# RWKV-7's chunked recurrence in 64x64 tiles of the array, both heads of a pair at once

## The chip, the cores and the metric

One core of one Trainium2 chip runs one launch of one decoder layer (batch 1, 1024 tokens, model width 1024, float32 in and out). The metric is the device time of the launch in microseconds (us).

## The reference

```python
for l in range(DEPTH):
    h = rms_norm(x, norm_mix_pre[l])
    proj = h @ w_in[l]                      # r,k,v and low ranks | S5 input | two gates
    o_rwkv = rwkv7_branch(...) @ w_branch_rwkv[l]
    o_s5 = s5_branch(...) @ w_branch_s5[l]
    mixed = (g_rwkv * o_rwkv + g_s5 * o_s5) @ w_out[l]
    x = x + rms_norm(mixed, norm_mix_post[l])
    f = conv_ffn(rms_norm(x, norm_ffn_pre[l]), ...)
    x = x + rms_norm(f, norm_ffn_post[l])
```

The part that matters is the recurrence inside rwkv7_branch, for 8 heads of width 64 (state S of 64x64 a head):

```python
def step(S, inp):
    r_t, w_t, k_t, v_t, a_t, b_t = inp
    sa = einsum('bhij,bhj->bhi', S, a_t)
    S = S * w_t[:, :, None, :] + sa[..., None] * b_t[:, :, None, :] + v_t[..., None] * k_t[:, :, None, :]
    return S, einsum('bhij,bhj->bhi', S, r_t)
```

## The kernel before

The layer runs in stages: input projection and the S5 scan, then the RWKV recurrence, then the merge, the output projection, the feed-forward part. Large products are split into three (high and low halves of both operands, lines 171 to 173, tile gm in the recurrence's stage).

**The recurrence.** The 1024 tokens go in two halves of 512 (th) and the 8 heads in four pairs of 128 channels; a unit d takes two pairs (u = 0, 1), so four heads, of one half. There are four units. A half has eight chunks (c) of 64 tokens. For each chunk the delta rule becomes products of 64x64 matrices: rwkv_front builds decayed rows ar (a part in columns 0 to 63, r part in 64 to 127) and bk (b part, k part), and the masked Gram matrices gr of bk with ar; the b-a block of gr has to be inverted (unit lower triangular). The inverse goes in blocks of 32: rwkv_inv takes the 32x32 diagonal blocks through DRAM (md, xd) and solves them in 62 VectorE steps; rwkv_level joins two blocks by two small products (lines 783, 786). rwkv_nat turns bk and v into token-major layout (lines 731, 738, 740). rwkv_chain then walks the eight chunks: state products (814), products with v (816), the solve (824), the outputs (828) and the new state (832, 835). rwkv_out is the layer norm and the gate.

In the kernel before, U (the solved rows, partitions 0 to 63) and v (partitions 64 to 127) share the tile UV, so one product over 128 rows takes both; gr has the b part on partitions 0 to 63 and the k part on 64 to 127, for both heads of a pair alike. Products are written to chk (two banks of PSUM) and chb.

**What sets the order.** TensorE's order is the order of emission. A planner (`drive`) walks lanes, which are generators: one chain lane (rwkv_nat, rwkv_level, rwkv_chain, rwkv_out of unit after unit) and two preparing lanes (rwkv_front of u = 0 and 1, then rwkv_inv). A lane yields (its cost in us, the wait until it may go on, a factor). Between a lane's steps the planner issues background steps of 0.68 us, three products each (gates, then merge and output projection): as many as the wait asks for, and as the lane's cost times 0.8 asks for. The other engines' queues are ordered by the framework by priority, and each runs in order.

```python
T_KN, T_BK, T_GR, T_INV, T_LV, T_CH, T_LN = 5.0, 9.0, 2.5, 36.0, 1.0, 0.8, 11.0
```

Of the kernel before, what the change touches and what calls it, by code (L numbers as in the profile page):

```python
# [9 lines left out]
F32 = mybir.dt.float32  # L10
# [3 lines left out]
ALU = mybir.AluOpType  # L14
# [10 lines left out]
CDEC = math.exp(-0.5)  # L25
MAGIC = 1.5 * 2.0 ** 23
# [44 lines left out]
class Kern:  # L71
# [569 lines left out]
    def rwkv_front(self, d, u):  # L641

        nc, V, G, A = self.nc, self.nc.vector, self.nc.gpsimd, self.nc.scalar
        mm = nc.tensor.matmul
# [51 lines left out]
        for q in range(2):  # L696
            ps = [self.rp((128, 4, 128)) for h in range(2)]
            for c in range(4 * q, 4 * q + 4):
                for h, sl in ((0, slice(0, 64)), (1, slice(64, 128))):
                    mm(ps[h][:, c % 4], bk[sl, c], ar[sl, c], start=c % 4 == 0, stop=True, skip_group_check=True)  # L700
            for h in range(2):
                V.tensor_tensor(d["gr"][:, u, 4 * q:4 * q + 4, h], ps[h], gm, ALU.mult)
            yield 1.8, T_GR
        g16 = d["gr"][:, u].rearrange("p c h t -> p (c h) t")
        for blk in range(2):
            sl = slice(32 * blk, 32 * blk + 32)
            nc.gpsimd.dma_start(d["md"][u, blk].rearrange("c q t -> q c t"), g16[sl, :, sl])
# [9 lines left out]
    def rwkv_nat(self, d):  # L717

        nc, A = self.nc, self.nc.scalar
        mm = nc.tensor.matmul  # L720
        ident = self.cst("ident")
        o = slice(d["th"] * 512, d["th"] * 512 + 512)
        d["bkn"] = self.tg("bkn", 1, (128, 2, 8, 128))
        d["UV"] = self.tg("UV", 1, (128, 8, 2, 2, 64))
        nc.gpsimd.memset(d["UV"][0:64], 0.0)
        for u in range(2):
            v = d["v"][u]
            for q in range(2):
                ps = self.rp((128, 4, 128))
                for c in range(4):  # L730
                    nc.tensor.transpose(ps[:, c], d["bk"][:, u, 4 * q + c], ident)
                A.copy(d["bkn"][:, u, 4 * q:4 * q + 4], ps)
                yield 0.5, 0
                ps = self.rp((128, 4, 128))
                for c in range(4):
                    b = 4 * q + c
                    if b == 0:
                        mm(ps[64:128, c], v[:, 0:64], ident, start=True, stop=True, skip_group_check=True)
                    else:
                        nc.tensor.transpose(ps[:, c], v[:, 64 * b - 64:64 * b + 64], ident)  # L740
                A.copy(d["UV"][64:128, 4 * q:4 * q + 4, :, u], ps[64:128].rearrange("p c (h i) -> p c h i", i=64))
                yield 0.5, 0.8

    def rwkv_inv(self, d):
# [19 lines left out]
        for u in range(2):  # L764
            xd = xds[:, u]

            g16 = d["gr"][:, u].rearrange("p c h t -> p (c h) t")
            for blk in range(2):
                sl = slice(32 * blk, 32 * blk + 32)
                nc.gpsimd.dma_start(g16[sl, :, sl], xd[16 * blk:16 * blk + 16].rearrange("c s r t -> (s r) c t"))  # L770

    def rwkv_level(self, d):
# [3 lines left out]
        g16 = [d["gr"][:, u].rearrange("p c h t -> p (c h) t") for u in range(2)]  # L776
        p0 = self.chk(1).rearrange("p (u c t) -> p u c t", u=2, t=32)
        p0, p1 = [p0[:, u] for u in range(2)], [self.chb().rearrange("p (c t) -> p c t", t=32) for u in range(2)]
        xz = [self.tg("ld", NLD)[0:64].rearrange("p (c t) -> p c t", t=32) for u in range(2)]
        for u in range(2):  # L780
            V.transpose(xz[u][0:32], g16[u][0:32, :, 0:32])
        yield 0, T_LT
        steps = ((lambda u, c: mm(p1[u][32:64, c], g16[u][0:32, c, 32:64], xz[u][0:32, c], start=c == 0, stop=True,
                                  skip_group_check=True),
                  lambda u: A.copy(xz[u][32:64], p1[u][32:64])),
                 (lambda u, c: mm(p0[u][0:32, c], xz[u][32:64, c], g16[u][32:64, c, 32:64], start=c == 0, stop=True,
                                  skip_group_check=True),
                  lambda u: A.copy(g16[u][0:32, :, 32:64], p0[u][0:32])))
        for step, evict in steps:
            for u in range(2):  # L790
                for c in range(16):
                    step(u, c)
                    if c % 8 == 7:
                        yield 0.4, 0.3, 4.5
                evict(u)
            yield 0, T_LV

    def rwkv_chain(self, d):
# [3 lines left out]
        S, pt, UV, gr, ar, bkn = self.S[d["g"]], d["pt"], d["UV"], d["gr"], d["ar"], d["bkn"]  # L802
        d["yn"] = self.tg("yn", 1, (128, 4, 2, 2, 64))
        kw = dict(stop=True, skip_group_check=True)
        uh = [(u, h) for h in range(2) for u in range(2)]
        for c in range(8):
            py = self.chk(1).rearrange("p (h n) -> p h n", h=2)[:, :, 0:128].rearrange("p h (u i) -> p h u i", i=64)
            cb = self.chb()
            pu = cb[0:64, 0:256].rearrange("p (h u i) -> p h u i", u=2, i=64)
            psn = cb[:, 256:384].rearrange("p (u i) -> p u i", i=64)  # L810
            for u in range(2):
                for h in (1, 0):
                    sl = slice(64 * h, 64 * h + 64)
                    mm(py[:, h, u], ar[sl, u, c], S[sl, u], start=u == 0, **kw)
            for u, h in uh:
                mm(py[0:64, h, u], gr[:, u, c, h, 0:64], UV[:, c, h, u], start=False, **kw)
            p1 = self.small.tile([64, 2, 2, 64], F32, tag="p1", name=self.nm("p1"), bufs=1)
            A.copy(p1, py[0:64])
# [3 lines left out]
            yield 1.25, T_CH  # L822
            for j, (u, h) in enumerate(uh):
                mm(pu[:, h, u], gr[0:64, u, c, h, 0:64], p1[:, h, u], start=j == 0, **kw)
            V.tensor_copy(UV[0:64, c], pu)
            yield 0.5, T_CH
            for u, h in uh:
                mm(py[64:128, h, u], gr[:, u, c, h, 64:128], UV[:, c, h, u], start=False, **kw)
            o = 64 * (c % 2)
            A.copy(d["yn"][o:o + 64, c // 2].rearrange("p u h i -> p h u i"), py[64:128])  # L830
            for u, h in uh:
                mm(psn[64 * h:64 * h + 64, u], bkn[:, u, c, 64 * h:64 * h + 64], UV[:, c, h, u],
                   start=u == 0 and h == 1, **kw)
            for u in range(2):
                V.scalar_tensor_tensor(S[:, u], psn[:, u], pt[:, c, u:u + 1], spt[:, u], ALU.mult, ALU.add)
            yield 0.9, T_CH
# [1008 lines left out]
```

## Time and profile before

| | |
|---|---|
| time, median of 3 runs | 1641.32 us |
| runs | 1638.31 to 1647.14 us |
| span of the profiled execution | 1644.6 us |
| instructions in it | 22694 |

The profiled execution is one more run of the same program; its own time is its span, 1644.6 us. Its page lists busy times of the engines: PE is the matrix engine, PEld its weight loads, DVE the vector engine, ACT the scalar engine, POOL GpSimd, SP the queue that issues most transfers. "L814" is line 814 of the kernel before. In the timeline a row has the start in us from the span's beginning, the duration in us, engine, line, operation, tiles (out<-in), then rows*columns of the array and the shape, and the number of instructions merged into the row. A row of groups has busy time and mean ns of one, then the engine's idle time before them and who ended it. A row of waits has who waited for whom, us in total, times, and the longest. A float32 matmul shows as two instructions, each with its own weight load.

### The profile page before, as it was taken

Reading aid. Unit: us, or ns where it says so; the run is one execution under the profiler, and the core shown is the slowest. Engines: PE = TensorE matmul, PEld = TensorE weight load, DVE = VectorE, ACT = ScalarE, POOL = GpSimd, SP = SyncE. Lnnn points to the kernel's source line nnn. Section 1 sums busy time; section 2 is a strip of 40 time slices with the busy share of each in tenths; the row PEclk is TensorE's granted clock in tenths of the full one; section 3 lists DMA queues with packets and bytes.
Section 4 is the critical chain, followed back from the end, with each engine's and each line's share of the span. In section 5 each row is a group of like instructions: output and inputs, shape, how many; then the busy total and the mean of one; then the engine's idle time right before and its main releaser. Section 6 shows DMA issues by size and latency. Waiting matters only on the chain. (4 is left out here: it accounts for less than half of the span.)

```text
span 1644.6 us, 22694 instructions
## 1 busy us (share of the span) xinstructions
PE 1542.0 (94%) x8372; PEld 1240.8 (75%) x8372; DVE 1132.4 (69%) x2035; ACT 699.6 (43%) x1069; POOL 134.6 (8%) x190
## 2 busy tenths in 40 slices
PE   5899899899999998988999899999999999999995
PEld 4688787687777776666777688888888887788784
DVE  5898764555456456584379668977777777788667
ACT  4345543133243244344344445544454454443451
POOL 2100101312113123010000000000000000000000
PEclk9799999999999999998999999999999999999998
DMA  5254244333342354462167454322222224963632
GB/s 174 68 148 144 86 141 140 99 106 116 96 144 91 97 164 132 126 186 70 54 189 259 155 165 144 128 88 90 77 77 90 89 78 132 318 222 97 218 95 102
DMA packets 132382, 213.63 MB, mean 130 GB/s; under 512 B 38144, under 2 KB 44288, under 8 KB 132272
## 3 DMA queue, kind: packets, MB, share of 16 engines
q1 hardware_dynamic: 124208, 188.32, 36.6%
q0 software_dynamic: 6912, 21.77, 4.5%
q10 hardware_dynamic: 1152, 2.10, 0.3%
q8 instruction: 66, 1.08, 0.3%
q14 instruction: 44, 0.36, 0.1%
HBM read 156.56 MB, written 53.48 MB: 128 GB/s over the span
## 5 line engine op out<-in xcount | busy, mean ns | idle before, releaser
L171 PE MATMUL gm<-hh,wh 128*128 128x512 f32 x688 | 297.7, 433 | 8.6 <-ACT hh L225 4.2
L172 PE MATMUL gm<-hl,wh 128*128 128x512 f32 x688 | 276.2, 401 | 5.3 <-DVE hl L226 4.4
L173 PE MATMUL gm<-hh,wl 128*128 128x512 f32 x688 | 274.7, 399 | 0.0
L155 ACT CAST wh<-wf 128x512 fp32r<-128x512 f32 x179 | 111.0, 621 | 232.1 <-PE gm L172 147.3
L156 DVE TENSOR_TENSOR wl<-wf,wh 128x512 fp32r<-128x512 f32 x179 | 124.3, 695 | 113.5 <-ACT wh L155 109.4
L171 PEld LDWEIGHTS gm<-hh,wh 128*128 128x128 f32 x688 | 132.3, 192 | 45.1 <-ACT hh L225 6.2
L172 PEld LDWEIGHTS gm<-hl,wh 128*128 128x128 f32 x688 | 133.0, 193 | 32.0 <-DVE hl L226 7.3
L173 PEld LDWEIGHTS gm<-hh,wl 128*128 128x128 f32 x688 | 132.7, 193 | 29.3
L1470 PE MATMUL d<-xl,wh 128*128 128x512 f32 x308 | 121.0, 393 | 5.7 <-DVE xl L226 5.7
L1469 PE MATMUL d<-xh,wh 128*128 128x512 f32 x308 | 120.8, 392 | 2.1 <-ACT xh L225 2.1
L1471 PE MATMUL d<-xh,wl 128*128 128x512 f32 x308 | 120.5, 391 | 0.0
L1295 PE MATMUL rp<-t,h 128*128 128x512 f32 x216 | 84.4, 391 | 2.0 <-ACT p L1309 2.0
L1297 PE MATMUL rp<-t,l 128*128 128x512 f32 x216 | 84.2, 390 | 0.5 <-DVE l L226 0.5
L1296 PE MATMUL rp<-t,h 128*128 128x512 f32 x216 | 84.1, 389 | 0.0
L1470 PEld LDWEIGHTS d<-xl,wh 128*128 128x128 f32 x308 | 58.1, 189 | 19.4 <-DVE xl L226 7.4
L1469 PEld LDWEIGHTS d<-xh,wh 128*128 128x128 f32 x308 | 58.2, 189 | 14.6 <-ACT xh L225 2.4
L1471 PEld LDWEIGHTS d<-xh,wl 128*128 128x128 f32 x308 | 58.2, 189 | 12.0
L225 ACT CAST h<-r 128x1024 fp32r<-128x1024 f32 x34 | 35.9, 1055 | 61.1 <-PE rp L1296 29.6
L226 DVE TENSOR_TENSOR l<-r,h 128x1024 fp32r<-128x1024 f32 x34 | 41.7, 1225 | 29.3 <-ACT h L225 27.7
L1316 DVE SCALAR_TENSOR_TENSOR y<-zv,vecs,y 128x1023 f32<-128x1023 f32 (+1 forms) x36 | 46.1, 1280 | 8.6 <-ACT y L1314 8.6
L1295 PEld LDWEIGHTS rp<-t,h 128*128 128x128 f32 x216 | 40.5, 188 | 11.5 <-ACT p L1309 2.8
L1297 PEld LDWEIGHTS rp<-t,l 128*128 128x128 f32 x216 | 40.5, 188 | 9.4 <-DVE l L226 1.0
(435 smaller groups left out, 3358.9 us busy)
## 6 DMA issues: line engine op xcount, KB each, us to landing
r<-in_w_up_dram SPq DMA_DIRECT2D x36, 512.0 KB, 3.7
wf<-in_w_in_dram SPq DMA_DIRECT2D x68, 256.0 KB, 3.1
st<-in_w_down_dram SPq DMA_DIRECT2D x55, 256.0 KB, 4.3
st<-ACT SPq DMA_DIRECT2D x44, 256.0 KB, 4.7
wf<-in_w_up_dram SPq DMA_DIRECT2D x36, 256.0 KB, 2.8
ACT<-y POOLq DMA_DIRECT2D x18, 512.0 KB, 2.9
GT<-ev SPq DMA_DIRECT2D x32, 256.0 KB, 2.0
wf<-in_w_br_dram SPq DMA_DIRECT2D x32, 256.0 KB, 2.9
```

The costliest lines, as they stand in the source:

```text
L155: nc.scalar.copy(h[:, :n], f[:, :n])
L156: nc.vector.tensor_tensor(l[:, :n], f[:, :n], h[:, :n].bitcast(F32), ALU.subtract)
L171: mm(ps, a, xh[k], start=k == 0, stop=False)
L172: mm(ps, a, xl[k], start=False, stop=False)
L173: mm(ps, b, xh[k], start=False, stop=k == n - 1)
L1295: mm(ps, wh[:, c], xh, start=first and k == 0, stop=False, skip_group_check=True)
L1296: mm(ps, wh[:, c], xl, start=False, stop=False, skip_group_check=True)
L1297: mm(ps, wl[:, c], xh, start=False, stop=k == 3, skip_group_check=True)
L1316: V.scalar_tensor_tensor(y[:, lag:], z[:, 0:1024 - lag], self.vec(nme, i), y[:, lag:], ALU.mult, ALU.add)
L1469: mm(ps, wh[:, c], xh[:, x], start=start, stop=False, skip_group_check=True)
L1470: mm(ps, wh[:, c], xl[:, x], start=False, stop=False, skip_group_check=True)
L1471: mm(ps, wl[:, c], xh[:, x], start=False, stop=stop, skip_group_check=True)
```

## The change

The two heads of a pair are mirrored over the partitions: head 0 keeps the b part of gr and bkn on partitions 0 to 63 and the k part on 64 to 127, head 1 has them the other way round. Each product of the recurrence becomes a 64x64 tile of the array, and the two heads and two halves (k = 0, 1) address the array's four quadrants. U and v get tiles of their own (U on its head's half, V on the other half); the products with v are in a new function, chain_v, which runs a chunk ahead of the rest of the chain: for chunk 0 at the start of rwkv_level, for chunk c + 1 right behind the solve of chunk c. They write a PSUM tile cz of two banks (two buffers), to which the later products of the chunk are added. rwkv_level treats both heads of all chunks in one group a u, in two 32x32 tiles. rwkv_nat uses products with the identity in 64x64 tiles in place of 128x128 transposes. The DMAs of diagonal blocks are one for each head and block, not one for each block. The planner's costs of these steps change with them.

```diff
+HALF = (slice(0, 64), slice(64, 128))
...
-    def chk(self, bufs=2):
-        return self.psx.tile([128, 1024], F32, tag="chk", name=self.nm("chk"), bufs=bufs)
-    def chb(self):
-        return self.psx.tile([128, 512], F32, tag="chb", name=self.nm("chb"), bufs=2)
+    def cz(self):
+        return self.psx.tile([128, 1024], F32, tag="cz", name=self.nm("cz"), bufs=2)
+    def chk(self):
+        return self.psx.tile([128, 1024], F32, tag="chk", name=self.nm("chk"), bufs=2)
...
-                for h, sl in ((0, slice(0, 64)), (1, slice(64, 128))):
-                    mm(ps[h][:, c % 4], bk[sl, c], ar[sl, c], start=c % 4 == 0, stop=True, skip_group_check=True)
+                for k in range(2):
+                    for h, sl in enumerate(HALF):
+                        mm(ps[h][HALF[h ^ k], c % 4], bk[sl, c, 64 * k:64 * k + 64], ar[sl, c], start=c % 4 == 0,
+                           stop=True, skip_group_check=True)
...
-        g16 = d["gr"][:, u].rearrange("p c h t -> p (c h) t")
         for blk in range(2):
-            sl = slice(32 * blk, 32 * blk + 32)
-            nc.gpsimd.dma_start(d["md"][u, blk].rearrange("c q t -> q c t"), g16[sl, :, sl])
+            for h in range(2):
+                o = 64 * h + 32 * blk
+                nc.gpsimd.dma_start(d["md"][u, blk].rearrange("(c h) q t -> h q c t", h=2)[h],
+                                    d["gr"][o:o + 32, u, :, h, 32 * blk:32 * blk + 32])
...
+            ps = [self.rp((128, 8, 64)) for h in range(2)]
+            for c in range(8):
+                for k in range(2):
+                    for h, sl in enumerate(HALF):
+                        mm(ps[h][HALF[h ^ k], c], d["bk"][sl, u, c, 64 * k:64 * k + 64], ident[sl, sl], start=c == 0,
+                           stop=True, skip_group_check=True)
+            for h in range(2):
+                A.copy(d["bkn"][:, u, :, h], ps[h])
+            yield 1.0, 0.3
+            ps = self.rp((128, 8, 64))
             v = d["v"][u]
...
+            for c in range(8):
+                for h, sl in enumerate(HALF):
+                    mm(ps[HALF[1 - h], c], v[sl, 64 * c:64 * c + 64], ident[sl, sl], start=c == 0, stop=True,
+                       skip_group_check=True)
+            A.copy(d["V"][:, :, u], ps)
+            yield 1.0, 0.8
...
+                for h in range(2):
+                    o = 64 * h + 32 * blk
+                    nc.gpsimd.dma_start(d["gr"][o:o + 32, u, :, h, 32 * blk:32 * blk + 32], xd[h])
...
+        p = self.cz().rearrange("p (u k c t) -> p u k c t", u=2, k=2, t=32)
+        xz = self.tg("ld", NLD).rearrange("p (u c t) -> p u c t", u=2, t=32)
+        lo, hi = (slice(0, 32), slice(64, 96)), (slice(32, 64), slice(96, 128))
         for u in range(2):
...
+            for h in range(2):
+                V.transpose(xz[lo[h], u], gr[lo[h], u, :, h, 0:32])
+        self.chain_v(d, 0)
+        yield 0.7, T_LT
+        for u in range(2):
+            for c in range(8):
+                for h in range(2):
+                    mm(p[hi[h], u, 0, c], gr[lo[h], u, c, h, 32:64], xz[lo[h], u, c], start=c == 0, **kw)
+            for h in range(2):
+                A.copy(xz[hi[h], u], p[hi[h], u, 0])
+            yield 0.6, 0.3, 2.5
+        yield 0, T_LV
+        for u in range(2):
+            for c in range(8):
+                for h in range(2):
+                    mm(p[lo[h], u, 1, c], xz[hi[h], u, c], gr[hi[h], u, c, h, 32:64], start=c == 0, **kw)
+            for h in range(2):
+                A.copy(gr[lo[h], u, :, h, 32:64], p[lo[h], u, 1])
+            yield 0.6, 0.3, 2.5
+        yield 0, T_LV
+
+    def chain_v(self, d, c):
+        mm = self.nc.tensor.matmul
+        V, gr, bkn = d["V"], d["gr"], d["bkn"]
+        z = d["z", c] = self.cz().rearrange("p (k n u i) -> p k n u i", k=2, n=4, i=64)
+        kw = dict(stop=True, skip_group_check=True)
+        for u in range(2):
+            for h, own in enumerate(HALF):
+                sl = HALF[1 - h]
+                mm(z[own, 0, 0, u], gr[sl, u, c, h, 0:64], V[sl, c, u], start=u == 0, **kw)
+                mm(z[sl, 1, 0, u], gr[sl, u, c, h, 64:128], V[sl, c, u], start=u == 0, **kw)
+            for h, own in enumerate(HALF):
+                sl = HALF[1 - h]
+                mm(z[own, 0, 1, u], bkn[sl, u, c, h], V[sl, c, u], start=False, **kw)
...
         for c in range(8):
+            z = d.pop(("z", c))
             for u in range(2):
+                for k in range(2):
+                    for h, sl in enumerate(HALF):
+                        mm(z[HALF[h ^ k], k, 0, u], ar[sl, u, c, 64 * k:64 * k + 64], S[sl, u], **kw)
+            p1 = self.small.tile([128, 2, 64], F32, tag="p1", name=self.nm("p1"), bufs=1)
+            A.copy(p1, z[:, 0, 0])
...
-            yield 1.25, T_CH
+            yield 0.6, T_CH
+            for u in range(2):
+                for h, sl in enumerate(HALF):
+                    mm(z[sl, 0, 2, u], gr[sl, u, c, h, 0:64], p1[sl, u], **kw)
+            U = self.small.tile([128, 2, 64], F32, tag="U", name=self.nm("U"), bufs=1)
+            V.tensor_copy(U, z[:, 0, 2])
+            if c < 7:
+                self.chain_v(d, c + 1)
+            yield 1.0, T_CH
+            for u in range(2):
+                for h, sl in enumerate(HALF):
+                    mm(z[sl, 0, 1, u], bkn[sl, u, c, h], U[sl, u], **kw)
+                for h, sl in enumerate(HALF):
+                    mm(z[HALF[1 - h], 1, 0, u], gr[sl, u, c, h, 64:128], U[sl, u], **kw)
+            for u in range(2):
+                V.scalar_tensor_tensor(S[:, u], z[:, 0, 1, u], pt[:, c, u:u + 1], spt[:, u], ALU.mult, ALU.add)
             o = 64 * (c % 2)
-            A.copy(d["yn"][o:o + 64, c // 2].rearrange("p u h i -> p h u i"), py[64:128])
+            for h in range(2):
+                A.copy(d["yn"][o:o + 64, c // 2, :, h], z[HALF[1 - h], 1, 0])
+            yield 0.6, T_CH
```

More of the change, by code (lines that the diff above doesn't have):

```diff
@@ L789, in rwkv_level @@
[L789 to L796, printed above, removed]
+            for h in range(2):
[10 more added lines that the diff above has]
+            yield 0.6, 0.3, 2.5
```

68 lines of the change are left out of this document (7 added, 61 removed).

## The prediction

> **What bounds the kernel now.** I read the page's totals first, then the table by stage over the recurrence, then TensorE's timeline of one chunk of the chain, then single groups of each line that changes.
>
> The page's first lines:
>
> ```profile
> span 1644.6 us, 22694 instructions
> ...
> PE 1542.0 (94%) x8372; PEld 1240.8 (75%) x8372; DVE 1132.4 (69%) x2035; ACT 699.6 (43%) x1069; POOL 134.6 (8%) x190
> ```
>
> The stages of the recurrence (columns: stretch, its length, busy time and instructions of PE, its weight loads, DVE, ACT, POOL; then granted clock, DMA share, GB/s):
>
> ```profile
> 390.00:480.00 90.00, 89.16 (x656) 67.83 (x655) 52.93 (x149) 28.43 (x61) 18.70 (x24) 1.00 0.32 97
> ...
> 700.00:764.00 64.00, 52.87 (x330) 39.95 (x326) 46.60 (x105) 30.82 (x50) 6.95 (x9) 0.87 0.53 145
> 764.00:822.00 58.00, 58.00 (x460) 43.39 (x460) 18.28 (x40) 22.58 (x53) 0.00 (x0) 1.00 0.19 56
> ```
>
> The last pair of heads runs its eight chunks in 764 to 822, with TensorE busy all the time at full clock, DVE for 18.28 us of 58 and ACT for 22.58. Only 700 to 764, between two chains, has holes. So time taken from TensorE's own stream in these stages shortens the run, as long as the other engines keep up. A busy TensorE can still be draining, so I take costs from starts. One chunk of that chain:
>
> ```profile
> 763.98 0.66 PE L814 MATMUL chk<-S,ar 64*128 64x64 f32 x8
> ...
> 766.44 0.40 PE L173 MATMUL gm<-hh,wl 128*128 128x512 f32 x1
> 766.77 0.68 PE L824 MATMUL chb<-p,gr 64*64 64x64 f32 x8
> 767.37 0.50 PE L171 MATMUL gm<-hh,wh 128*128 128x512 f32 x1
> 767.71 0.39 PE L172 MATMUL gm<-hl,wh 128*128 128x512 f32 x1
> ...
> 768.96 0.50 PE L828 MATMUL chk<-UV,gr 128*64 128x64 f32 x5
> 769.25 0.27 PE L832 MATMUL chb<-UV,bkn 128*64 128x64 f32 x1
> 769.30 0.22 PE L828 MATMUL chk<-UV,gr 128*64 128x64 f32 x1
> 769.36 0.22 PE L832 MATMUL chb<-UV,bkn 128*64 128x64 f32 x1
> 769.36 0.22 PE L828 MATMUL chk<-UV,gr 128*64 128x64 f32 x1
> ...
> 769.47 0.40 PE L832 MATMUL chb<-UV,bkn 128*64 128x64 f32 x5
> 769.80 0.50 PE L171 MATMUL gm<-hh,wh 128*128 128x512 f32 x1
> ...
> 771.39 0.33 PE L814 MATMUL chk<-S,ar 64*128 64x64 f32 x2
> ```
>
> and the background products alone:
>
> ```profile
> 344.25 0.39 PE L171 MATMUL gm<-hh,wh 128*128 128x512 f32 x1
> ...
> 344.93 0.39 PE L171 MATMUL gm<-hh,wh 128*128 128x512 f32 x1
> ```
>
> A background step (three products) takes 344.93 - 344.25 = 0.68, or 0.227 a product. A chunk is 771.39 - 763.98 = 7.41 with six such steps (4.08), so the chain's own 20 products (40 instructions: a float32 product is two) cost 3.33 a chunk, and 32 chunks 107 us. The line L824 calibrates the parts. Between L173 at 766.44 and L172 at 767.71 lie 1.27, of which two pitches (0.455) are the background's: 0.815 for eight instructions in one 64x64 tile. They start 0.058 apart (0.60 over eight, with about 0.15 of it leaving the mode): 8 x 0.058 = 0.46 is streaming, and **0.35 is the price of entering and leaving another tile mode**. The Trainium skill, "TensorEngine Tiling (Array Packing)", Key Properties, says that a changed tiling mode drains the engine; the 0.35 agrees.
>
> L828 and L832 show the second fact. L828 fills the array's upper 64 columns, L832's first products the lower 64; they start in the same hundredth (769.36) while each keeps 0.058 within its own half. So tiles in other columns run at once, and a later instruction need not wait for an earlier one of another tile.
>
> **The change, part by part.** Three terms move, and I cost each as streaming plus 0.35 a visit.
>
> *Chain.* A 128-row product becomes two of 64x64, spread over four tiles: 20 products become 32, of which 12 (v's, in chain_v) are issued a chunk earlier, behind the p1 products. Three visits a chunk stay. If the four tiles run at once: state products, 16 instructions, 4 in each tile: 4 x 0.058 + 0.35 = 0.58. p1 with the next chunk's v: 32 instructions, at best 8 in a tile, at worst p1's 4 and then v's 8 in a row: 0.81 to 1.05, and I take 0.93, the middle, since p1 uses two tiles and part of v the other two. Last visit 0.58. Sum 2.09 against 3.33: 1.24 a chunk, 32 chunks, -39.7. The last chunk of each of four pairs has no v behind it (-0.35 x 4 = -1.4); the first chunk's v is a visit of its own in the level stage (8 x 0.058 + 0.35 = 0.81, four times, +3.2). Chain: **-37.9**.
>
> *Level.* One of its groups now:
>
> ```profile
> 384.45 0.39 PE L173 MATMUL gm<-hh,wl 128*128 128x512 f32 x1
> 384.77 0.69 PE L786 MATMUL chk<-gr,ld 32*32 32x32 f32 x16
> 385.38 0.50 PE L171 MATMUL gm<-hh,wh 128*128 128x512 f32 x1
> 385.72 0.40 PE L172 MATMUL gm<-hl,wh 128*128 128x512 f32 x1
> ```
>
> 1.27 - 0.455 = 0.815 for 16 instructions in one 32x32 tile, 0.032 apart. There are eight groups a pair of heads, 6.5 us. After: four groups of 32 instructions in two tiles of other rows and columns: if they overlap, 16 x 0.032 and the visit again, 0.815 each, 3.3. **-13.0** for four (one after the other, 1.33 each, -4.8).
>
> *Natural layout (rwkv_nat).* Now transposes of 128x128, without a change of mode:
>
> ```profile
> 359.61 0.40 PE L173 MATMUL gm<-hh,wl 128*128 128x512 f32 x1
> 359.85 0.60 PE L731 MATMUL rp<-csts,bk 128*128 128x128 f32 x4
> 360.29 0.60 PE L740 MATMUL rp<-csts,ld 128*128 128x128 f32 x4
> 360.64 0.48 PE L171 MATMUL gm<-hh,wh 128*128 128x512 f32 x1
> 360.96 0.40 PE L172 MATMUL gm<-hl,wh 128*128 128x512 f32 x1
> ```
>
> 1.35 - 0.455 = 0.89 a group, two for each of eight blocks: 1.8 a block. After: true float32 products with the identity, 64 instructions over four tiles and 32 over two, 16 in a tile both times: 2 x (16 x 0.058 + 0.35) = 2.56. **+6.2**.
>
> *Gram products.*
>
> ```profile
> 311.05 0.40 PE L173 MATMUL gm<-hh,wl 128*128 128x512 f32 x1
> 311.37 1.16 PE L700 MATMUL rp<-ar,bk 64*128 64x128 f32 x16
> 312.46 0.50 PE L171 MATMUL gm<-hh,wh 128*128 128x512 f32 x1
> 312.80 0.39 PE L172 MATMUL gm<-hl,wh 128*128 128x512 f32 x1
> ```
>
> 1.75 - 0.455 = 1.30 for 16 instructions that stream 128 columns. The transposes above stream 128 columns 0.109 apart (0.44 for four), so 16 in a row would be 1.74 alone: the two row halves overlap already. After: 32 instructions, eight in each of four tiles, 8 x 0.109 + 0.35 = 1.22. I take 0; with only two tiles at a time it is 16 x 0.109 + 0.35 = 2.09, +0.8 in each of 16 groups, +12.6.
>
> *DVE, ACT and POOL.*
>
> ```profile
> L830 ACT COPY yn<-chk 64x256 f32<-64x256 f32 x32 | 11.8, 369 | 53.8 <-PE chk L828 53.6
> L707 POOL DMA_DIRECT2D md<-gr x16 | 10.6, 667 | 41.7 <-DVE gr L702 41.0 <-issue 0.7
> L770 POOL DMA_DIRECT2D gr<-xd x16 | 10.3, 654 | 12.2 <-DMA xd<-x 9.0 <-PE rp L740 3.2
> ```
>
> The copies of p1 and U go from 256 columns on 64 partitions to 128 on 128; yn's copy becomes two of half the width, the nat copies go from four to three, the transposes from two wide to four narrow, and UV's memset goes. I cost this at nothing: two background steps (1.36 us) still stand between the visits, and the engines are idle for over half of the chain. Without that cover the second yn copy costs at most 32 x 0.369 = 11.8. chain_v adds a wait: its PSUM buffer must be free of the chunk before last's yn copies and state update, and all of TensorE's stream, background included, stands behind it. Those readers were issued a visit and two background steps earlier, so nothing is charged; late, it costs a copy, 0.37.
>
> The stores to md and the loads of gr from xd are halved in height: 16 more issues each on POOL's queue. Between a pair's Gram products and its level lie two more of the first (1.3) and four more of the second (2.6): the level's input lands 3.9 later, and what POOL does for the next pair stands behind them. Meanwhile TensorE arrives earlier: with about half of a chain's chunks in that stretch, by 4 x 1.24 = 5.0. So up to 8.9 of slack goes in each of the three levels that follow a chain. What slack there is:
>
> ```profile
> PE chb L783 <- DVE ld L781: 5.1, 1, 5.1
> PE rp L861 <- DVE yn L855: 4.8, 1, 4.8
> PE chk L828 <- DVE UV L825: 4.7, 5, 1.8
> ```
>
> TensorE waits once for a level's input (the fourth level), once for the layer norm before it, and five times for U's copy, whose cover grows (v's products now stand behind p1's). The fourth has no slack, so all 8.9 comes back there; the other two never wait now, and I let them hide it. Ends: 0 and 3 x 8.9 = 27; I take **+9**.
>
> Sum: -37.9 - 13.0 + 6.2 + 0 + 9 = -35.7. The terms come from one execution of 1644.6, 3.3 over the median of 1641.32 (runs 1638.31 to 1647.14), so 1608.9 there and **1605** at the median.
>
> **Rivals.** *Full overlap, as summed:* 1605, from 1588 (p1 and v at 0.81, levels hidden, the 4.7 for U gone) to 1615 (two levels uncovered, 18). For it: L828 with L832 across columns, L700 across rows. Against it: no row has more than two tiles at work.
>
> *A floor on starts.* The densest stretch above is L828 with L832, two tiles at 0.058 each, so 0.029 a start. If no more can be issued, four tiles go at the speed of two: visits of 0.81, 1.28 and 0.81, -0.43 x 32 = -14; the first and last chunks together +1.4; levels 1.28 a group, -5.6; nat 3.49 a block, +13.5; Gram 0. Sum -4.5, with up to 4 of stalls **1637 to 1641**. The Trainium skill, "TensorE: Matmul & The Clock Gate", Part 1, states a floor of about 25 ns from start to start; by that figure the same sum would come to some 11 us less, an estimate. The same page's Part 3 has packed tiles starting about 4 ns apart. The pairs that start in the same hundredth agree with the latter, but two are not sixteen.
>
> *Slower: 64x64 tiles run one after the other.* L824, the only line in this mode, uses one tile alone and cannot exclude it. Then visits of 1.28, 2.21 and 1.28: +1.44 x 32 = +46; the first and last chunks +1; levels -4.8; nat 3.71 + 1.86 + 0.70 = 6.27 a block, +36; Gram 32 x 0.109 + 0.35 = 3.84, +41. Sum +119: **1760**. It decides from about 0.030 a start, averaged over tiles; two tiles give 0.029 in the rows at 769.36, so the change needs a third and a fourth to gain.
>
> *The gain turns into waits for the inverse.* The inverse runs on DVE and through DRAM, not on TensorE. If all three levels lack slack, with a pair's chain shortened by 10, 27 comes back and more at the layer norm (4.8 waited already): **1624 to 1632**.
>
> **How the numbers follow.** Full overlap 0.62, floor 0.16, waits 0.10, serial tiles 0.08, something unseen and slower 0.04. A measurement here tells about 0.5% (8.2 us) from no change, so faster is under 1633.1: 0.62, 0.09 of the waits and 0.02 of the floor, 0.73; same 0.15; slower 0.12. The range 1588 to 1640 holds all but the two slower cases and the edges of the others; full overlap alone has 1588 to 1615.
>
> **What would show it.** A chunk of the last chain at 6.1 to 6.3 us instead of 7.41; starts in all four tiles within 0.02 and next ones 0.058 later; a Gram group still 1.1 from first start to background; level groups of 32 in the 0.6 that 16 take; longer waits of L783's successor for the transposes. Wrong if p1 with v takes over 1.2 us (floor) or 2.2 (serial), or if TensorE's waits in 300 to 850 grow by more than 27.

## The result, and the profile after

The changed kernel takes 1635.72 us (median of its runs, 1631.04 to 1641.13) against 1643.74 for the kernel before in the same comparison (1638.31 to 1647.34): ratio 0.9958, 95% interval 0.9943 to 0.9973. So 0.4% faster, about 7 us, where the forecast said 2.2% (1605 us). The direction was right, and the time lies inside the range, but only because the range reached up to 1640, almost to the kernel before; four fifths of the gain are missing. The profiled execution spans 1638.7 us, 5.9 less than before.

The stretch of the recurrence as one window, in the kernel before and then in the changed kernel (columns as in the prediction's table by stage):

```profile
300.00:830.00 530.00, 504.40 (x3633) 385.00 (x3632) 291.34 (x722) 198.40 (x381) 88.31 (x118) 0.97 0.39 114
```

```profile
300.00:830.00 530.00, 479.10 (x5290) 358.58 (x5289) 290.24 (x748) 199.95 (x428) 102.23 (x147) 0.93 0.41 123
```

TensorE is busy for 25.3 us less, and its granted clock falls from 0.97 to 0.93. A clock of 0.93 over 530 us is 37 us of work lost to half clock, 0.97 is 16: at most 21 more, give or take 5 for the rounding, and some of it lies inside waits.

The last pair's chain, from TensorE's timeline (the starts of its first and second chunks, three visits from the fourth to the fifth, the start of the eighth):

```profile
736.32 0.46 PE L832 MATMUL cz<-S,ar 64*64 64x64 f32 x16
...
742.68 0.46 PE L832 MATMUL cz<-S,ar 64*64 64x64 f32 x16
...
757.12 0.40 PE L174 MATMUL gm<-hh,wl 128*128 128x512 f32 x1
757.45 0.27 PE L841 MATMUL cz<-p,gr 64*64 64x64 f32 x2
757.48 0.27 PE L814 MATMUL cz<-V,gr 64*64 64x64 f32 x1
...
758.57 0.40 PE L173 MATMUL gm<-hl,wh 128*128 128x512 f32 x1
...
759.52 0.39 PE L174 MATMUL gm<-hh,wl 128*128 128x512 f32 x1
759.84 0.27 PE L849 MATMUL cz<-U,bkn 64*64 64x64 f32 x2
759.85 0.27 PE L851 MATMUL cz<-U,gr 64*64 64x64 f32 x2
...
760.57 0.40 PE L173 MATMUL gm<-hl,wh 128*128 128x512 f32 x1
...
761.51 0.39 PE L174 MATMUL gm<-hh,wl 128*128 128x512 f32 x1
...
762.56 0.40 PE L173 MATMUL gm<-hl,wh 128*128 128x512 f32 x1
...
781.49 0.54 PE L832 MATMUL cz<-S,ar 64*64 64x64 f32 x16 [0.19 <-DVE S L853]
```

By the prediction's method (from L174 ahead of a visit to L173 behind it, less 0.455) the visits cost 0.995 (p1 with v), 0.595 and 0.595, 2.185 a chunk instead of 3.33; seven chunks take 781.49 - 736.32 = 45.2. Four tiles do run at once: L849 and L851 start 0.01 apart, and 16 instructions of L832 take 0.46. The level, the layout and the Gram products, in the same way:

```profile
377.01 0.39 PE L174 MATMUL gm<-hh,wl 128*128 128x512 f32 x1
377.33 0.69 PE L791 MATMUL cz<-ld,gr 32*32 32x32 f32 x32
...
378.29 0.40 PE L173 MATMUL gm<-hl,wh 128*128 128x512 f32 x1
```

```profile
357.79 0.39 PE L174 MATMUL gm<-hh,wl 128*128 128x512 f32 x1
358.11 1.16 PE L733 MATMUL rp<-csts,bk 64*64 64x64 f32 x64
...
359.54 0.39 PE L173 MATMUL gm<-hl,wh 128*128 128x512 f32 x1
359.77 0.40 PE L174 MATMUL gm<-hh,wl 128*128 128x512 f32 x1
360.09 1.15 PE L742 MATMUL rp<-csts,ld 64*64 64x64 f32 x32
...
361.50 0.39 PE L173 MATMUL gm<-hl,wh 128*128 128x512 f32 x1
```

```profile
314.64 0.39 PE L174 MATMUL gm<-hh,wl 128*128 128x512 f32 x1
314.96 1.10 PE L702 MATMUL rp<-ar,bk 64*64 64x128 f32 x32
...
316.33 0.40 PE L173 MATMUL gm<-hl,wh 128*128 128x512 f32 x1
```

A level's group takes 0.825, the two of a layout block 1.295 and 1.275, a Gram group 1.235. So TensorE's own terms came out at: chain 32 x 1.145 = -36.6, with the prediction's own figures for the ends (-1.4 and +3.2) -34.8; level 4 x (6.52 - 3.30) = -12.9; layout +6.3; Gram -1.0. Sum **-42.4**, where the prediction had -44.7. Whole chunks give a little less: the first one, which has no wait, takes 742.68 - 736.32 = 6.36 us against 7.41, so 1.05 a chunk in place of 1.145, and the sum is then some -39.

Yet the stage ends no earlier. The first product of the last merge, which follows the recurrence, in the kernel before and in the changed one:

```profile
830.69 0.39 PE L171 MATMUL gm<-e,wh 128*128 128x512 f32 x1
```

```profile
833.08 0.39 PE L172 MATMUL gm<-e,wh 128*128 128x512 f32 x1
```

All that TensorE's own terms saved is back by here. What TensorE waited for from 295 to 850 in the changed kernel (us, times, longest):

```profile
PE cz L832 <- DVE S L853: 12.4, 5, 4.3
PE cz L791 <- DVE ld L784: 6.0, 5, 2.1
PE gm L172 <- ACT hh L226: 5.8, 1, 5.8
PE cz L849 <- DVE U L843: 5.4, 4, 1.8
...
PE cz L791 <- ACT ld L793: 5.0, 1, 5.0
PE cz L799 <- ACT gr L801: 3.1, 3, 1.6
PE rp L742 <- ACT bkn L736: 3.1, 1, 3.1
```

All groups together are 53.7 us; in the kernel before they were 29.2. So 24.5 more waits, and up to 21 more of half clock: 45 against the 39 to 42 saved. The 6 us by which the whole execution is shorter come behind this point, some 5 in the merge stage up to 956 and 3 behind 1400, for a stage that ends 2.4 later; no run here was made on those two.

VectorE around the largest of these waits, with what TensorE did behind it:

```profile
398.42 1.86 DVE L713 SCALAR_TENSOR_TENSOR ld<-ld,vecs,ld 128x512 f32<-128x512 f32 x1 [1.96 <-POOL ld L691]
400.21 0.28 DVE L843 COPY U<-cz 128x128 f32<-128x128 f32 x1
...
403.84 1.85 DVE L713 SCALAR_TENSOR_TENSOR ld<-ld,vecs,ld 128x512 f32<-128x512 f32 x1 [2.02 <-POOL ld L691]
...
406.21 0.46 DVE L853 SCALAR_TENSOR_TENSOR S<-cz,pt,spt 128x64 f32<-128x64 f32 x2
```

```profile
400.55 0.27 PE L849 MATMUL cz<-U,bkn 64*64 64x64 f32 x2 [1.70 <-DVE U L843]
...
406.54 0.54 PE L832 MATMUL cz<-S,ar 64*64 64x64 f32 x16 [3.95 <-DVE S L853]
```

U's copy and the update of S stand in VectorE's queue behind L713, the bonus product r * r_k * ta of a preparing lane. L713 itself waits for GpSimd (L691) and then takes 1.86 us; nothing needs its result soon. In the kernel before the two lanes' products (L709) stood at 395.00 and 410.32; here they are 5.4 us apart and fall into one chunk.

### The profile page after: what moved, and what is told of

Same layout as the page of the kernel before. It is cut to its first block, busy times and chain, and to the rows that moved or that the text cites. A ratio compares the mean times of both kernels' runs of the same rounds, so it can differ in the third digit from the quotient of the medians.

```text
span 1638.7 us, 26115 instructions
## 1 busy us (share of the span) xinstructions
PE 1520.3 (93%) x10028; PEld 1218.0 (74%) x10028; DVE 1124.7 (69%) x2043; ACT 696.7 (43%) x1109; POOL 146.1 (9%) x218
## 5 line engine op out<-in xcount | busy, mean ns | idle before, releaser
L172 PE MATMUL gm<-hh,wh 128*128 128x512 f32 x688 | 302.2, 439 | 13.4 <-ACT hh L226 9.5
L173 PE MATMUL gm<-hl,wh 128*128 128x512 f32 x688 | 282.8, 411 | 7.6 <-DVE hl L227 5.0
L174 PE MATMUL gm<-hh,wl 128*128 128x512 f32 x688 | 280.2, 407 | 0.0
L172 PEld LDWEIGHTS gm<-hh,wh 128*128 128x128 f32 x688 | 135.9, 198 | 51.7 <-ACT hh L226 12.1
L173 PEld LDWEIGHTS gm<-hl,wh 128*128 128x128 f32 x688 | 136.7, 199 | 36.4 <-DVE hl L227 8.3
L174 PEld LDWEIGHTS gm<-hh,wl 128*128 128x128 f32 x688 | 136.5, 198 | 30.4
L837 ACT ACTIVATE spt<-S,pt 128x64 f32<-128x64 f32 x64 | 19.8, 342 | 78.2 <-DVE S L853 77.8
```

The lines of the kernel that those rows point to most:

```text
L172: mm(ps, a, xh[k], start=k == 0, stop=False)
L173: mm(ps, a, xl[k], start=False, stop=False)
L174: mm(ps, b, xh[k], start=False, stop=k == n - 1)
```

## The experiments

**1. The bonus product off VectorE's queue.** Theory: the saved time returns as waits behind queues that run in order. Rivals: the shortened chain itself follows too closely; or another engine becomes late.

```diff
-        V.scalar_tensor_tensor(r, r, self.vec("r_k", p), ta, ALU.mult, ALU.mult)
+        G.tensor_scalar(r, r, self.vec("r_k", p), self.cst("gmask")[:, 0:1], ALU.mult, ALU.add)
+        G.tensor_tensor(r, r, ta, ALU.mult)
```

> The changed kernel with one instruction of the preparing lanes moved: the product r * r_k * ta (L713) goes from VectorE to GpSimd, as two instructions. Theory (the time saved in TensorE's stream comes back as waits behind queues that run in order): in chunks 2 and 3 of pairs 0 to 2, L713 stands in VectorE's queue ahead of U's copy and the state's update, and waits there for GpSimd (L691). Without it TensorE's waits for U (2.1 to 2.2 us, three times) and for S (4.1 to 4.7 us, three times) go, 19 us in all, and with them the half clock that follows each: 15 to 27 us faster than the changed kernel, 1609 to 1621 us. Rival 1 (those waits come from the shortened chain itself: p1, U and S follow each other too closely for ScalarE and VectorE whatever stands ahead): the waits move to the next visit, under 4 us gained, 1632 to 1638. Rival 2 (GpSimd becomes late instead: bonus and Gram inputs come from one queue): new waits of TensorE for bk (L702) or for the bonus product, no gain or a loss of up to 10 us.

Measured: 1620.78 us, 0.9846 of the kernel before (0.9826 to 0.9866). TensorE's written order is the same as in the changed kernel. Its waits:

```profile
PE cz L792 <- DVE ld L785: 6.6, 4, 2.9
...
PE cz L833 <- DVE S L854: 1.3, 3, 0.9
...
PE cz L850 <- DVE U L844: 0.2, 1, 0.2
```

17.8 us of waits for S and U became 1.5, and the run is 1.1% (18 us) faster than the changed kernel. Theory held, and the first rival fell. What the second rival named did come, 4.0 us of waits for bk behind GpSimd (L692) where there had been none, but it cost less than the move saved: all waits together fell from 53.7 us to 39.7. The cause of these 18 us was one instruction in the wrong place of a queue.

**2. Control: the same move in the kernel before.**

> Control: the kernel before with the same move of the product r * r_k * ta to GpSimd. There the two lanes' products stand 15 us apart and TensorE waited for U by VectorE 4.7 us in all. Theory: at most those 4.7 us and 3 to 4 us of half clock, 0 to 8 us faster than the kernel before, so the move pays mainly in the changed kernel. Rival (VectorE is simply overloaded in both kernels, and any instruction taken from it pays): the same 15 to 27 us here.

1646.38 us, ratio 1.0005 (0.9990 to 1.0020): nothing. The waits for U by VectorE did not go (6.8 us, 4.7 before), and new ones for bk behind GpSimd came (4.4). So VectorE isn't overloaded as such, and the gain of experiment 1 belongs to the changed kernel.

**3. More background products in the level.**

```diff
-            yield 0.6, 0.3, 2.5
+            yield 0.8, 0.3, 4.5
```

> The changed kernel with the planner's figures of the level's groups raised (0.6 with factor 2.5 becomes 0.8 with factor 4.5), which asks for 11.5 us of background products a pair as the kernel before did, in place of 4.8. Theory: TensorE's waits inside the level (L791 for L793's copies, L799 for the xd loads, 1.0 to 5.0 each, some 12 us in all with the clock after them) shrink: 3 to 10 us faster than the changed kernel, 1626 to 1633. Rival (the level waits for its input, the inverse by VectorE and DRAM, at its entry, before these figures act): the entry waits at L784 (6.0 us) stay, 0 to 3 us gained.

1625.63 us, 0.9880 (0.9856 to 0.9904). More than expected, and not for the reason expected. In the profiled execution (1634.61 us, the slowest of six) waits at the transposes fell from 6.0 to 1.0, but those for S fell too, from 12.4 to 5.7, and a new one for the layer norm came (9.2). The planner's figure moves all lanes against each other, so one figure tests no single cause.

**4. The chain's planner figures of before** (0.6, 1.0, 0.6 back to 1.25, 0.5, 0.9).

> The changed kernel with the planner's figures of the chain set back to those of the kernel before (1.25, 0.5, 0.9 in place of 0.6, 1.0, 0.6). These decide how the two preparing lanes fall between the visits of the chain. Theory: the waits for U and S come from how closely the two preparing lanes run (their L713 are 5.4 us apart, 15 us before); if the old figures put them apart again, part of the 19 us of waits goes, 5 to 15 us faster than the changed kernel; if they leave the lanes side by side, no change within 3 us. Rival (the chain's own steps follow too closely, and the figures add nothing between them since two background steps stand there anyhow): no change within 3 us, with the lanes apart and the waits still there.

1630.50 us, 0.9902 (0.9879 to 0.9925): 9 us, within the theory's range, but not by its way. The two L713 of the first chain still stand 6.0 us apart (396.57 and 402.59). They fall at other places of the chunk: the waits for S went from 12.4 to 5.1, those for U from 5.4 to 4.4.

**5. Experiments 1 and 3 together.**

> Both edits at once: the bonus product on GpSimd (e1_bonus_pool, 0.9846 of the kernel before) and more background products in the level (e3_level_fill, 0.9880; the changed kernel alone 0.9958). Theory (each wait has its own cause and its own cover): the gains of 18 and 13 us add up in large part, 0.976 to 0.980, 1607 to 1613. Rival (both edits only push the same loose lanes apart; what e3 gained was its drop of TensorE's waits for S from 12.4 to 5.7, which e1 has already): no more than 3 us over e1, 0.983 to 0.985.

1626.62 us, 0.9875 (0.9852 to 0.9899): no better than experiment 1 alone, if anything worse. This fits the rival, which took e3's gain for the same one that experiment 1 has. What came in place, for the layer norm and for the buffer that chain_v needs:

```profile
PE rp L883 <- DVE yn L877: 9.4, 3, 8.0
PE cz L815 <- ACT yn L857: 6.3, 3, 3.8
```

**6. The chain's lane six us later** (experiment 1 with `T_INV` 36 raised to 42).

> e1_bonus_pool with the planner's time for the inverse (T_INV) raised from 36 to 42, so the chain's lane starts each pair later by 6 us of background products. Theory: TensorE arrives at the level before its input (6.6 us of waits at L785 for the transposes, which wait for the loads of gr from xd); with the later start these go, and with them their half clock: 4 to 10 us faster than e1, 1611 to 1617. Rival (the start of a pair sets the end of the stage: a later start is a later end): each of the pairs whose inverse was late before moves the end by up to 6 us, no change to 12 us slower than e1.

1616.99 us, 0.9821 (0.9795 to 0.9847); the interval overlaps that of experiment 1. The waits at the transposes went (6.6 to 0.9), others grew (L794 9.6, layer norm 8.0). Not told apart.

**7. Half of the level's loads on another queue** (experiment 1, and in `rwkv_inv`):

```diff
-                    nc.gpsimd.dma_start(d["gr"][o:o + 32, u, :, h, 32 * blk:32 * blk + 32], xd[h])
+                    (nc.sync if h else nc.gpsimd).dma_start(d["gr"][o:o + 32, u, :, h, 32 * blk:32 * blk + 32], xd[h])
```

> e1_bonus_pool with four of the eight loads of gr from xd per pair issued by SyncE in place of GpSimd. The change doubled these loads (2.57 us of issue for the stores, 4.62 for the loads on GpSimd at 574.84 in e1_bonus_pool, the last transposes 4.8 after the end of the issues). Theory of the doubled issues: with half of them on another queue the input of the level lands some 2 us sooner, the 6.6 us of waits at L785 shrink to 2 or less, 2 to 6 us faster than e1. Rival (SyncE's queue runs in order too, and its stores of GT wait for the gate's tiles, up to 9 us at 659.50 in the changed kernel): the loads get stuck there, waits at L785 as long or longer, 0 to 15 us slower.

1609.91 us, 0.9775 (0.9752 to 0.9799): 0.7% or some 11 us faster than experiment 1, about twice the most that was expected. SyncE didn't get stuck. Waits and window:

```profile
PE cz L792 <- DVE ld L785: 3.1, 3, 1.6
```

```profile
300.00:830.00 530.00, 493.02 (x5410) 368.60 (x5409) 305.11 (x775) 214.22 (x451) 110.52 (x145) 0.96 0.45 135
```

The waits at L785 fell by 3.5, and the clock rose to 0.96 (0.94 in experiment 1), worth some 10 us over the 530. ScalarE's written order also differs at 24 places from experiment 1, and VectorE's differs too, so this run doesn't say how much is the loads alone.

**8. The price of a wait.** Experiment 1 with idle work behind U's copy:

```diff
             V.tensor_copy(U, z[:, 0, 2])
+            if d is self.ds[3] and c % 2:
+                for _ in range(24):
+                    V.tensor_scalar(U, U, 1.0, None, ALU.mult)
```

> The price of a wait, measured: e1_bonus_pool with 24 more VectorE instructions (times 1.0, 128x128) behind U's copy in the chunks 1, 3, 5 and 7 of the last pair's chain, which has no waits for VectorE in e1. Each chain of 24 takes some 5 us, of which 2 lie beside background and v's products (beside background alone in chunk 7): four waits of about 3 us at L850, 13 us in all. Theory: each wait is followed by 3.4 to 6.8 us at half the granted clock, which costs 1.7 to 3.4 more: 20 to 27 us slower than e1 in all. Rival (the clock is a matter of load over a longer time, not of single waits): 12 to 14 us slower, and no half clock in that stretch.

1654.54 us, 1.0051 (1.0035 to 1.0067), 2.05% or 34 us over experiment 1 (give or take 4). The waits were twice as long as planned, and what follows the first of them can be read from TensorE's timeline:

```profile
PE cz L853 <- DVE U L847: 27.6, 4, 7.3
```

```profile
728.15 0.37 PE L853 MATMUL cz<-U,bkn 64*64 64x64 f32 x2 [7.32 <-DVE U L847]
...
729.38 0.63 PE L173 MATMUL gm<-hl,wh 128*128 128x512 f32 x1
729.80 0.63 PE L174 MATMUL gm<-hh,wl 128*128 128x512 f32 x1
...
733.66 0.39 PE L172 MATMUL gm<-hh,wh 128*128 128x512 f32 x1
733.89 0.39 PE L173 MATMUL gm<-hl,wh 128*128 128x512 f32 x1
```

Background products start 0.43 apart instead of 0.23 until about 733.3, 5.2 us after the wait, which costs some 2.5. Behind the four waits the granted clock is 0.50 for 5.4, 4.2, 3.2 and 6.0 us, which costs 1.6 to 3.0 each and 9.4 in all, as the theory has it. In time the four waits cost 27.6 and about 6 more (give or take 4), 1.5 each; experiment 1 has some 3 us of half clock of its own around 696 to 713 that this run has not. So the half clock is real, and it follows single waits. The Trainium skill, "TensorE: Matmul & The Clock Gate", Part 1 (HAM oscillation), puts the penalty at half of the throttled time; the pitches here, 0.43 against 0.23, agree.

**9. Control: both edits of experiment 7 in the kernel before.**

> Control: the kernel before with both edits of e7_bonus_sp_loads (the bonus product on GpSimd, half of the loads of gr from xd on SyncE; two of four per pair here). e2_before_bonus_pool stood at 1.0005. Theory (the edits remove waits that the changed kernel has and the kernel before hardly has): TensorE waited there once for the level's input (5.1 us), so 0.994 to 1.001, 1635 to 1647, and the array tiles are worth the difference to e7 (0.9775), 28 us or more. Rival (the loads by SyncE are good for any kernel): the same 0.993 to 0.990 that e7 gained over e1.

1639.51 us, 0.9964 (0.9947 to 0.9981). The second queue helps the kernel before a little as well. With the same two edits in both, the change as a whole (the array tiles and the new order that comes with them) is worth 0.9775 / 0.9964 = 0.981, **31 us**, give or take 5.

**10. The loads alone, bonus product left on VectorE.**

> The changed kernel with half of the loads of gr from xd on SyncE, and the bonus product left on VectorE. e7 gained 0.7% by this over e1. Theory (two separate causes): the waits for U and S stay (17.8 us in the changed kernel), those at L784 (6.0) shrink; 0.988 to 0.991, 5 to 12 us faster than the changed kernel. Rival (the loads only help once the chain no longer waits): within 3 us of the changed kernel, 0.994 to 0.998.

1626.20 us, 0.9889 (0.9866 to 0.9911), 0.7% faster than the changed kernel as in experiment 7 over 1, with the waits for S and U left (10.7 and 6.1). The two causes are separate, and their gains add up.

**11. The first merge's loads of YR on GpSimd's queue** (on experiment 7).

> e7_bonus_sp_loads with the four loads of YR at the start of the first merge on GpSimd's queue. In the changed kernel TensorE waits once there, 5.8 us for hh (L226; 7.0 in e7), because the loads stand in SyncE's queue behind a store of GT that waits 9 us for its tile. Theory: the wait goes or falls under 2 us, and half clock of 3.4 us with it: 4 to 9 us faster than e7, 1600 to 1606. Rival (the loads are late because the merge itself comes at that time, or because their buffers come free only then): no change within 3 us.

1610.13 us, 0.9793 (0.9768 to 0.9817): no gain over experiment 7. The loads now go out 25 us ahead of the merge, and the wait for hh fell from 7.0 to 2.6, but what was late next takes its place, the same merge's hl and the layer norm:

```profile
PE rp L883 <- DVE yn L877: 6.3, 3, 4.6
...
PE gm L173 <- DVE hl L227: 2.8, 1, 2.8
PE gm L172 <- ACT hh L226: 2.6, 1, 2.6
```

**12. v's products in a visit of their own** (on experiment 7).

```diff
             V.tensor_copy(U, z[:, 0, 2])
+            yield 0.6, T_CH / 2
             if c < 7:
                 self.chain_v(d, c + 1)
-            yield 1.0, T_CH
+            yield 0.4, T_CH / 2
```

> e7_bonus_sp_loads with v's products of the next chunk in a visit of their own, one background step behind the p1 products and one ahead of U's, in place of the same visit as p1's. Theory (a visit in another tile mode costs 0.35 us to enter and leave, and TensorE's stream is what bounds these stages): 28 more visits, and streams that no longer overlap: 0.58 and 0.81 in place of 0.93, so 28 x 0.46 = 13 us slower than e7 if p1 and v shared a visit as I took them, 10 if only the 0.35 counts. Rival (there is slack now, and another stop gives the copies of U more cover): within 4 us of e7.

1622.09 us, 0.9861 (0.9836 to 0.9886): 0.86% or 14 us slower than experiment 7, with about the same sum of waits (35.9 against 36.6). That agrees with the 13 worked out, but at give or take 6 it can't be told from the 10. TensorE's timeline has p1 alone at 0.585 (from 714.58 to 715.62, less 0.455) and v alone at 0.825 (from 715.86 to 717.14), 1.41 in place of 0.995: 28 x 0.415 = 11.6 us. The mean clock over 300 to 830 is 0.95 against 0.96, so some of the 14 can be that. The price of a visit stands, and work added to TensorE's stream shows in the time. Products of v in the chunk's own first visit, or in the last visit of the chunk before, weren't tried.

**13. The doubled DMA issues alone, in the kernel before.** Each store to md and load of gr is cut into two of 16 partitions:

```diff
-                nc.gpsimd.dma_start(g16[sl, :, sl], xd[16 * blk:16 * blk + 16].rearrange("c s r t -> (s r) c t"))
+                for i in range(2):
+                    hq = slice(32 * blk + 16 * i, 32 * blk + 16 * i + 16)
+                    nc.gpsimd.dma_start(g16[hq, :, sl], xd[16 * blk:16 * blk + 16].rearrange("c s r t -> (s r) c t")[16 * i:16 * i + 16])
```

> The kernel before with one part of the change alone: the stores of gr to md and the loads of gr from xd cut into twice as many, of half the height, all on GpSimd's queue as in the changed kernel; no array tiles. Theory (the doubled issues are a cost of their own): each level's input lands about 4 us later; the fourth level, which waits already (5.1 us at L783), waits some 4 longer, the others have slack: 2 to 8 us slower than the kernel before, 1.001 to 1.005. Rival 1 (no level has slack to hide it): three to four times 4 us, 1.007 to 1.010. Rival 2 (the issues do not matter; what e7 gained over e1 is the second queue, since e9 gained 0.4% on the kernel before too): 0.999 to 1.001, waits at the transposes as before.

1677.60 us, ratio 1.0222 (1.0191 to 1.0253): 36 us slower, beyond every expectation. The wait for the level's input:

```profile
PE chb L787 <- DVE ld L785: 17.3, 6, 7.6
```

It goes from 5.1, once, to 17.3, six times, and the mean clock over 300 to 830 from 0.97 to 0.94 (some 16 us of work): 12 and 16 of the 36. All four levels waited, the first, which follows no chain, among them, so none had the slack that the theory counted on. Behind the wait from 493.26 to 496.01 (2.75 us) the granted clock is 0.50 from 496.3 to 513.3. But the cut also shifts what else stands where: TensorE's written order is unchanged, VectorE's differs at 153 places. So it shows how dear a late level is, not that the issues alone cost 36 us.

**14. The chain's planner figures of before, on experiment 7.**

> e7_bonus_sp_loads with the chain's planner figures of the kernel before (1.25, 0.5, 0.9), which by themselves gained 0.56% on the changed kernel (e4). Theory (e4 gained by moving the preparing lanes apart, so that less of L713's wait fell on U and S, which e7 has removed at its cause): no more gain, within 4 us of e7, 0.975 to 0.980. Rival (the old figures put the lanes in better places altogether): 6 to 9 us faster than e7, 0.972 to 0.974.

1619.53 us, 0.9847 (0.9822 to 0.9871), 0.7% slower than experiment 7. Both expectations missed: what gained 0.56% on the changed kernel loses here, with waits of 6.5 for L794 and 6.1 for bk (L692) in place of 3.3 and 4.0. A planner's figure has no price of its own.

**15. The copy that sets up the inverse's x on GpSimd** (`A.copy(x, ...)` becomes `nc.gpsimd.tensor_copy(x, ...)`, on experiment 7).

> e7_bonus_sp_loads with the copy that sets up the inverse's x (L755) on GpSimd in place of ScalarE. In e1 it stood in ScalarE's queue ahead of bkn's copies, waited 4.66 us for the store of the last x, and TensorE behind it waited 2.9 us for bkn (L737); 1.5 in e7. Theory (same pattern as L713: an instruction that waits, ahead of one that TensorE needs): this wait goes and the half clock after it with it, 2 to 5 us faster than e7. Rival (the copies of bkn are late because ScalarE has just too much to copy at that place): no change within 2 us, the wait for bkn as long.

1605.40 us, 0.9777 (0.9750 to 0.9803): level with experiment 7. The wait for bkn is gone (1.5 before), as the theory said, but the waits at the transposes rose from 3.1 to 5.0.

**16. Half of the stores to md on SyncE too** (on experiment 7), **and 15 with it.**

> e7_bonus_sp_loads with the stores of gr to md, also doubled by the change, split the same way: half on SyncE. Theory (e13 showed the doubled issues cost 2.2% on the kernel before; the stores stand ahead of the inverse, so their 2.35 us of issue in place of 1.3 make the whole inverse later): the inverse starts about 1 us sooner and the level's input comes as much sooner, waits at L785 and the clock after them shrink: 2 to 6 us faster than e7, 0.974 to 0.976. Rival (SyncE's queue stands behind stores of GT at these places, and the inverse starts later): 0 to 10 us slower than e7.

> e17_both_md_sp with the copy of the inverse's x on GpSimd as in e15_both_xinit_pool (which was level with e7). Theory: level with e17 within 4 us. Rival (GpSimd, freed of half the issues, takes the copy at no cost and the level's wait for bkn goes too): 3 to 6 us faster than e17.

1605.91 us, 0.9746 (0.9722 to 0.9769), and 1606.63 us, 0.9769 (0.9742 to 0.9795). Neither can be told from experiment 7. Experiments 7, 11, 15 and these two lie from 0.975 to 0.979, faster than both kernels.

## Why the prediction was wrong, step by step

- *Price of a visit, four tiles at once:* right. 0.595 for 0.58, 0.995 for 0.93; experiment 12 agrees in time (14, give or take 6, for 13). The floor on starts and the serial tiles fell.
- *Chain -37.9, level -13.0, layout +6.2, Gram 0:* measured -34.8, -12.9, +6.3, -1.0. The miss is 0.095 a chunk in the chain, 0.065 of it p1 with v.
- *A chunk of the last chain at 6.1 to 6.3:* 6.36 without a wait, 45.2 / 7 = 6.45 on the mean of seven, both a little above it. The visits alone would give 2.185 + 4.08 = 6.27.
- *"DVE, ACT and POOL ... I cost this at nothing":* **the first step that failed.** The cover was counted as two background steps between visits and engines idle over half of the time. An engine's idle share says nothing where its queue runs in order: an instruction of the preparing lane that waits blocks the chain's behind it. That was worth 18 us (experiment 1). I had looked at the last chain, which has no preparing lanes beside it; three of the four have.
- *"I take +9" for stalls (ends 0 to 27):* **the second.** The waits grew by 24.5, near the upper end, but not at the three levels alone: S and U 13.1 more, ScalarE's copies in the level 7.5 more, the first merge 5.8, bkn 3.1, while those for the Gram matrices and the layer norm fell by 5.8. The level's input (+0.9) is hardly more in the sum, yet moving half of its loads gave 0.7%.
- *Half clock:* no term at all, though the table by stage showed 0.87 between two chains. Long waits drag half clock behind them, up to 21 us more than before here. Short ones alone need not: after the wait of 1.82 us that ends at 676.49 in the kernel before, the clock is 1.00 up to 690. In the level it lasts longer than behind experiment 8's waits: after 1.94 and 2.08 us of waits up to 599.02 in the changed kernel the granted clock is 0.50 up to 612.5, which costs 6.7 us. No run here says why. Without that term the condition "waits grow by more than 27" was set too high: 24.5 were enough.
- *The rival "gain turns into waits for the inverse" (0.10, 1624 to 1632)* came nearest in kind; its place was wrong, since most waits were not for the inverse.
- *"Some 11 us less"* in the floor's rival: the same sums give about 13; no other number rests on it.

With the two queues relieved (experiment 7) the time is 1609.91, and the stage ends at

```profile
799.17 0.39 PE L172 MATMUL gm<-e,wh 128*128 128x512 f32 x1
```

31.5 us earlier than before. So most of the stream's saving is there to be had; what was wrong was to take it as free of the queues.

Left open: how much of experiment 7's gain is the number of issues and how much the order that came with it, why the half clock lasts longest in the levels, and why experiment 13 costs as much as it does.

## What to carry to other kernels

When TensorE's work shrinks between steps that depend on one another, look at each in-order queue in the stretch where other work runs beside it, not in the quiet one, and move what waits there and is not needed soon. Price a new wait of several us at its length and the half clock behind it, here 1.6 to 3.0 us in a chain and 6.7 in one level. A gain read off one engine's stream is what can be had at most; what a change is worth shows only with the same edits in the kernel before as a control.

## What was not expected of the hardware

Tiles of 64x64 start closer than the prediction's rows had shown: 64 instructions of L733 in 1.16 us are 0.018 a start, and the timeline has instructions of several tiles in one hundredth (757.74 in the same chunk). A later product of another tile starts ahead of an earlier one: L814 at 757.48 with six of L841's still to come. L713 takes 1.86 us on VectorE, where a product of the same size beside it (L688 at 394.58) takes 0.68. GpSimd works at the same time (L692, from 398.47, for 1.27). The kernel before has the same instruction as L709: it took 0.74 the one time that GpSimd's product (L691, from 511.80 for 1.30) ended 0.05 us after its start at 513.05, and 1.85 to 1.88 the other seven times, beside the whole of L691. So the product beside it on GpSimd makes it slow, as far as these traces show; no run here moved that product alone.
